# Row sums of squared differences on one core: two first loads of x instead of four, and the result stored in two halves from two queues

## The chip, the core and the metric

The kernel runs on one core of a Trainium2 chip. The metric is the device time of one execution in microseconds. Before the change it is 84.13 us, the median of three runs (84.11 to 84.14).

## What is computed

Two float32 arrays of 1024 x 4096 come in; for each row the sum of the squared differences goes out, 1024 float32 values.

```python
def reference(x, y, axis):          # x, y: (1024, 4096) float32, axis = -1
    return np.sum((x - y) ** 2, axis=axis).astype(np.float32)
```

Each input is 16.8 MB, so 33.55 MB are read and 4 KB are written. Nothing is read twice.

## The kernel before

Each of the 128 partitions holds R = 8 rows of D = 4096 elements, so x and y are each seen as 128 x 32768 (lines 60 and 61), and a partition's share is one contiguous stretch of memory. The work goes along these 32768 columns. On the chip, X and Y each have room for 24576 columns (`H = 6 * D`); the columns above that are written over those of the first two rows once these have been squared.

**Loads.** `xw` and `yw` (lines 72 and 73) are the widths of the pieces in which x and y are loaded; one piece is one DMA of 128 partitions (`load`, line 108) with a semaphore of its own. All loads are issued by SP, on one queue, in the order of the list `order`: before each piece of y come the pieces of x that it needs. The first piece of y is 16256 columns wide, so the first four pieces of x (512, 1536, 4096 and 10240 columns, together 16384) stand ahead of it. These four are issued "early": `prog.early` moves them ahead of SP's Drain in the entry block, that is ahead of the barriers with which the program begins. The barriers let the other engines go on only when SP has come to them. The first piece of y and the later loads follow behind the barriers. As many loads as fit into the room are issued at once (up to the 8192-column pieces); the rest are issued when the square of the last piece of row 0, and then of row 1, is done (line 221 is SP's wait). SP's queue holds only so many transfers: an issue into a full queue lasts until there is room.

**Work.** For each piece of y, in order, DVE waits for the piece and for the pieces of x that it needs (`wait_loaded`, line 172), subtracts it from x in place (line 176), cut at the rows' ends and for some pieces halved. ACT squares each difference and adds it up along the row into one column of `parts` (line 182). A row that was done in several pieces is summed by DVE at its end (line 189). The very last piece, 128 columns, is squared on DVE itself (line 205), and then row 7 is summed. The semaphore `diffs` counts DVE's subtractions, `acts` ACT's squares, `sums` the results that are final.

**Store.** When all results are final, SP issues one DMA of 128 partitions x 8 values (line 233), with the semaphore `stored`. `close` clears the program's semaphores (line 44) and waits for `stored` (line 45). That wait is the last instruction of the program.

Engine names: DVE is VectorE, ACT is ScalarE, SP is SyncE, POOL is GpSimd. Line numbers are those of the kernel before.

Of the kernel before, what the change touches and what calls it, by code (L numbers as in the profile page):

```python
# [47 lines left out]
def kernel(tc, x, y, axis, out):  # L48
    nc = tc.nc
    P = nc.NUM_PARTITIONS  # L50
# [11 lines left out]
    ov = out.rearrange("(p r) -> p r", p=P)  # L62
# [5 lines left out]
    results = nc.alloc_sbuf_tensor("results", [P, R], F32).ap()  # L68

    xw = [512, 1536, 4096, 10240, 8192, 5472, 1280, 960, 320, 160]
    yw = [16256, 8192, 2624, 2784, 1344, 480, 480, 288]
    late, last = 128, 192
    LATE = 3
# [15 lines left out]
    prog = Program(nc, tc)  # L91
    stored = nc.alloc_semaphore("stored")
    diffs = prog.semaphore("diffs")
    acts = prog.semaphore("acts")
    sums = prog.semaphore("sums")
    n = dict(diffs=0, acts=0, sums=0)

    def home(c0, c1):
        h0 = c0 % H
        return slice(h0, h0 + c1 - c0)  # L100
# [5 lines left out]
    def load(landed, src, dst, name, c0, c1):  # L106
        sem = prog.semaphore("%s%d" % (name, len(landed)))
        nc.sync.dma_start(out=dst[:, home(c0, c1)], in_=src[:, c0:c1]).then_inc(sem, 16)  # L108
        landed.append(((c0, c1), sem))
# [7 lines left out]
        order.append((landed_y, yv, Y, "y", c0, c1))  # L117

    todo = list(order)
    for _ in range(4):  # L120
        load(*todo.pop(0))
    prog.early(mybir.EngineType.SP)
    while todo and todo[0][5] <= H:
# [63 lines left out]
    def complete(r):  # L187
        nc.vector.wait_ge(acts, squared[row_parts[r][-1]])
        nc.vector.tensor_reduce(  # L189
            out=results[:, r : r + 1],  # L190
            in_=parts_of(r, len(row_parts[r])),
            axis=mybir.AxisListType.X,
            op=add,
        ).then_inc(sums, 1)
        n["sums"] += 1

    for j, (c0, c1) in enumerate(ys):
        final = j == len(ys) - 1
        wait_loaded(c1, landed_y[j][1])
        for piece in pieces_of(j, c0, c1):  # L200
            sub(*piece)
            r = piece[0] // D
            if final:
                nc.vector.wait_ge(diffs, n["diffs"])
                nc.vector.tensor_tensor_reduce(  # L205
                    out=Y[:, home(*piece)],
# [22 lines left out]
                complete(r)  # L229
    complete(7)  # L230

    nc.sync.wait_ge(sums, n["sums"])
    nc.sync.dma_start(out=ov, in_=results).then_inc(stored, 16)
    prog.close(nc.sync, stored, 16)


# [33 lines left out]
```

## Time and profile before

| | |
|---|---|
| time of the profiled execution | 84.13 us |
| its span, first to last instruction | 82.80 us |
| around the span | 1.33 us |
| first load issued by SP | 0.00 us |
| the four early loads, from first issue to end of the last | 1.80 us |
| first load of y issued | 2.86 us |
| first subtraction on DVE | 41.04 us |
| one subtraction of 128 x 4096 | 4.42 us |
| one square of 128 x 4096 | 3.62 us |
| last subtraction ends | 80.82 us |
| store issued | 81.36 us |
| issue to landing of the store | 1.4 us |

All times within the execution count from the start of the span. The trace also has a record of every DMA packet: its start, its length and its size, not the engine that moved it. A load of 128 partitions appears as 128 packets, 8 for each of the 16 DMA engines, with one completion of 4 bytes for each engine behind them. In the chain that ended last, an entry "DMA Y<-in_y_dram" is the time from the issue of such a load to its landing, and "SPq" is time in which SP issued or waited.

### The profile page before, as it was taken

To read this page: it belongs to the slowest core of one execution; us is meant where nothing else is said; L and a number is where in the kernel's file an instruction comes from. 1 tells how busy PE (TensorE), PEld (TensorE's weight loads), DVE (VectorE), ACT (ScalarE), POOL (GpSimd) and SP (SyncE) were. 2 spreads that over 40 slices of the span, in tenths; PEclk is the share of its full clock that TensorE was granted. 3 is DMA by queue.
4 is the path that set the end of the run, shared out by engine and by line. 5 is a ranking of instruction groups with operands and counts; after the bars stand their busy time and mean duration, and the time that the engine had idled before them with its cause. 6 is when DMAs were issued, how large, how long until landed. Compare 5 with 4: busy or idle time off the path is not lost.

```text
span 82.8 us, 139 instructions
## 1 busy us (share of the span) xinstructions
DVE 36.8 (44%) x27; ACT 33.4 (40%) x41; POOL 0.2 (0%) x4
## 2 busy tenths in 40 slices
DVE  0000000000000000000199999999179996989992
ACT  0600000000000000000000979889796999899991
POOL 0000000000000000000000000000000000000000
DMA  5999997997999995699699989979999999999950
GB/s 137 393 452 419 455 613 317 396 554 317 503 503 503 503 503 220 283 503 503 285 475 507 412 348 507 443 332 491 412 391 465 389 411 424 430 408 416 395 195 2
DMA packets 3024, 33.56 MB, mean 405 GB/s; under 512 B 464, under 2 KB 1360, under 8 KB 2000
## 3 DMA queue, kind: packets, MB, share of 16 engines
q1 hardware_dynamic: 3024, 33.56, 95.7%
HBM read 33.55 MB, written 0.00 MB: 405 GB/s over the span
## 4 chain that ended last, share of the span: by engine, by line
DMA 59%; SPq 19%; DVE 12%; ACT 4%; issue 1%
DMA Y<-in_y_dram 59%; SPq L108 19%; DVE X L176 11%; ACT X L182 4%; DVE Y L205 0%; DVE results L189 0%; SPq L221 0%; DVE results L205 0%
## 5 line engine op out<-in xcount | busy, mean ns | idle before, releaser
L176 DVE TENSOR_TENSOR X<-X,Y 128x2048 f32<-128x2048 f32 (+10 forms) x21 | 36.3, 1779 | 44.5 <-DMA Y<-in_y_dram 44.3
L182 ACT ACTIVATE X<-X 128x2048 f32<-128x2048 f32 (+9 forms) x20 | 31.2, 1558 | 44.8 <-DVE X L176 44.8
L182 ACT ACTIVATION_READ_ACCUMULATOR X<-X 128x1 f32 x20 | 3.7, 186 | 0.0
L182 ACT ACT_TABLE_LOAD x1 | 1.3, 1283 | 2.9 <-PEq L19 2.9
L189 DVE TENSOR_REDUCE results<-parts 128x1 f32<-128x2 f32 (+2 forms) x4 | 0.4, 151 | 0.0
L205 DVE CUSTOM_DVE_ANT_0 Y<-X,parts 128x128 f32<-128x128 f32 x1 | 0.4, 353 | 0.0
L251 POOL MEMSET const-bfloat16-1.0<- 128x1 bf16 x1 | 0.1, 101 | 0.0
L251 POOL MEMSET const-uint8-127<- 128x1 uint8 x1 | 0.1, 101 | 0.0
L251 POOL MEMSET const-float32-0.0<- 128x1 f32 x1 | 0.1, 98 | 0.2 <-issue 0.2
L251 POOL MEMSET const-float32-1.0<- 128x1 f32 x1 | 0.1, 98 | 0.0
L205 DVE DVE_READ_ACCUMULATOR2_ANT results<- 128x1 f32 x1 | 0.1, 84 | 0.0
## 6 DMA issues: line engine op xcount, KB each, us to landing
Y<-in_y_dram SPq DMA_DIRECT2D x1, 8128.0 KB, 38.2
X<-in_x_dram SPq DMA_DIRECT2D x1, 5120.0 KB, 20.4
X<-in_x_dram SPq DMA_DIRECT2D x1, 4096.0 KB, 47.5
Y<-in_y_dram SPq DMA_DIRECT2D x1, 4096.0 KB, 56.7
X<-in_x_dram SPq DMA_DIRECT2D x1, 2736.0 KB, 13.3
X<-in_x_dram SPq DMA_DIRECT2D x1, 2048.0 KB, 8.8
Y<-in_y_dram SPq DMA_DIRECT2D x1, 1392.0 KB, 18.9
Y<-in_y_dram SPq DMA_DIRECT2D x1, 1312.0 KB, 16.1
```

Source lines behind the costliest of these rows:

```text
L108: nc.sync.dma_start(out=dst[:, home(c0, c1)], in_=src[:, c0:c1]).then_inc(sem, 16)
L176: nc.vector.tensor_sub(out=a, in0=a, in1=Y[:, home(c0, c1)]).then_inc(diffs, 1)
L182: nc.scalar.activation(out=a, in_=a, func=Square, accum_out=acc).then_inc(acts, 1)
L189: nc.vector.tensor_reduce(out=results[:, r : r + 1], in_=parts_of(r, len(row_parts[r])), axis=mybir.AxisListType.X, op=add,).then_inc(sums, 1)
L205: nc.vector.tensor_tensor_reduce(out=Y[:, home(*piece)], in0=X[:, home(*piece)], in1=X[:, home(*piece)], scale=1.0, scalar=parts_of(r, 1), ...
L251: nc = _bacc.Bacc("TRN2", target_bir_lowering=False, num_devices=1)
```

## The change

The four early loads of x become two, of 4096 and 12288 columns: the same 16384 columns, in the same place of the order. The store becomes two DMAs of 64 partitions: ACT issues the upper half and SP the lower half, each after its own wait for `sums`. ACT then increments a new semaphore, `begun`, and SP waits for it before the program's semaphores are cleared, among them `sums`, for which ACT waits. The last wait counts both halves (32 in place of 16).

```diff
-    xw = [512, 1536, 4096, 10240, 8192, 5472, 1280, 960, 320, 160]
+    xw = [4096, 12288, 8192, 5472, 1280, 960, 320, 160]
...
+    begun = prog.semaphore("begun")
...
-    for _ in range(4):
+    for _ in range(2):
         load(*todo.pop(0))
     prog.early(mybir.EngineType.SP)
...
+    half = P // 2
+    nc.scalar.wait_ge(sums, n["sums"])
+    nc.scalar.dma_start(out=ov[half:P], in_=results[half:P]).then_inc(stored, 16)
+    nc.scalar.sem_inc(begun, 1)
     nc.sync.wait_ge(sums, n["sums"])
-    nc.sync.dma_start(out=ov, in_=results).then_inc(stored, 16)
-    prog.close(nc.sync, stored, 16)
+    nc.sync.dma_start(out=ov[0:half], in_=results[0:half]).then_inc(stored, 16)
+    nc.sync.wait_ge(begun, 1)
+    prog.close(nc.sync, stored, 32)
```

## The prediction

> **What bounds the kernel now.** I read the page's engine shares and slices first, then the chain that ended last, then the transfers, and last the two places that the diff touches: the first microseconds and the end. The page:
>
> ```profile
> span 82.8 us, 139 instructions
> ...
> DVE 36.8 (44%) x27; ACT 33.4 (40%) x41; POOL 0.2 (0%) x4
> ...
> DMA  5999997997999995699699989979999999999950
> GB/s 137 393 452 419 455 613 317 396 554 317 503 503 503 503 503 220 283 503 503 285 475 507 412 348 507 443 332 491 412 391 465 389 411 424 430 408 416 395 195 2
> ...
> q1 hardware_dynamic: 3024, 33.56, 95.7%
> ...
> DMA 59%; SPq 19%; DVE 12%; ACT 4%; issue 1%
> ```
>
> No compute engine is busy half the time; the 16 DMA engines are busy 95.7% of it. So the time is: a start, 33.55 MB at a steady rate, and an end. The 19% of SPq in the chain is SP held in one issue (11.12 us from 58.42) because earlier transfers fill its queue; the transfers themselves go on meanwhile.
>
> The steady rate comes from two rows of the transfers:
>
> ```profile
> Y<-in_y_dram SPq DMA_DIRECT2D x1, 8128.0 KB, 38.2
> X<-in_x_dram SPq DMA_DIRECT2D x1, 5120.0 KB, 20.4
> ...
> out_dram<-results SPq DMA_DIRECT2D x1, 4.0 KB, 1.4
> ```
>
> The 5120 KB piece of x was issued at 1.37 us and landed at 21.8; the 8128 KB piece of y was issued at 2.86 and landed at 41.0, straight behind it. 8.323 MB in 19.2 us is 433 GB/s. At that rate the first 8.389 MB (the x columns of the edit) need 19.4 us, yet they landed at 21.8: the stream is 2.4 us late. Of this, 1.0 us lies ahead of the first packet (issue at 0.00, first packet in the trace's packet records at 1.00) and 0.37 us between an engine's last packet and its completion. The remaining **1.07 us** is all that any other order of loads could recover. The windows show where it goes (start:end, length, the engines' busy time, clock, DMA share, GB/s):
>
> ```profile
> 0.90:1.30 0.40, 0.00 (x0) 0.00 (x0) 0.00 (x0) 1.00 0.75 133
> 1.30:1.70 0.40, 0.00 (x0) 0.00 (x0) 0.00 (x0) 1.00 0.61 179
> 1.70:2.10 0.40, 0.00 (x0) 0.00 (x0) 0.00 (x0) 1.00 1.42 425
> 2.10:2.50 0.40, 0.00 (x0) 0.00 (x0) 0.00 (x0) 1.00 0.86 271
> 2.50:2.90 0.40, 0.00 (x0) 0.04 (x1) 0.00 (x0) 1.00 0.90 369
> ...
> 9.00:21.00 12.00, 0.00 (x0) 0.00 (x0) 0.00 (x0) 1.00 1.00 434
> ```
>
> Two dips: 133 and 179 GB/s while the 512-column load runs, and 271 as the 1536-column load begins.
>
> The end, from the chain in order of time and the timeline:
>
> ```profile
> 69.58 10.65 DMA Y<-in_y_dram
> 80.23 0.02 issue
> 80.25 0.57 DVE X L176 x2
> 80.83 0.03 issue
> 80.85 0.35 DVE Y L205
> ...
> 81.36 0.35 SPq L233 DMA_DIRECT2D out_dram<-results  x1
> ```
>
> The last loads land, 1.1 us of compute follows, the store is issued at 81.36 and is home 1.4 us later. The profiled execution took 84.13 us for a span of 82.80, so 1.33 us lie around it; its time equals the median of the three runs, and I take every sum from 84.13.
>
> **The loads, removed part.** Two of four early loads go; the bytes stay. (a) In the packet records each load gives each DMA engine 8 packets and one completion. Undisturbed packets start 80 ns apart at 2 KB, 231 ns at 6 KB, 607 ns at 16 KB: 27.2 bytes per ns plus 4.7 ns a packet; a completion adds 6 ns. A load fewer saves 8 x 4.7 + 6 = 44 ns on each engine, two save **0.09 us**.
>
> (b) Some early packets are far slower: 2 KB ones take up to 539 ns against a usual 84, 6 KB ones up to 989 against 234. Summed over what is usual and divided by 16 engines, that is 0.22 us per engine in the first load, 0.24 in the second, 0.02 in the third. Later small packets (512 to 1920 bytes at the end) have none of it. The trace can't say whether the excess belongs to the small early loads or to the first microseconds of reading. Bounds: all 0.46 goes, or all stays, or a first load of 16 KB rows is worse still: if the dip of 0.9 to 1.7 us (156 GB/s on average) also filled 1.7 to 2.5, where 348 were moved, 0.8 x (348 - 156) / 433 = 0.36 us more are lost. I take **0.24**: the second load's excess goes, since most of its slow packets are the first of that load, and with 4096 columns first the next load begins only near 6 us, when the third load of now shows almost nothing; the first load's stays, since some first load must meet the cold start. A large first row could also hide its stall, as one 16 KB packet covers 607 ns; this I leave for a rival.
>
> (c) SP's early block ends sooner: the removed issues stood 0.47 us apart, so SP's drain, now at 1.85 us, comes near 0.9. The other engines reach that barrier by 0.5 us, so the barriers, the table load of ACT (now at 2.86) and the first load of y (2.86) all move some 0.9 us forward. Worth nothing: that load queues behind 19 us of x, and ACT has nothing to square before 45 us. DVE has two waits fewer in a stretch where it idles until 41.04. The queue that holds SP later holds it as before, and the load so held lands at 79.98, 10 us after SP began to issue it.
>
> **Does an earlier stream reach the end?** DVE waits for DMA before the pieces of 2048, 1312 and 736 columns (idle 2.13, 0.77 and 0.36 us), and its last subtractions begin 0.02 us after landings at 79.73 and 80.23. Every run of compute thus hangs on a landing and moves with it; up to about 0.36 us nothing else is late instead. Beyond that the 736-column run starts to lean on DVE.
>
> **The store, added part.** Now: issue 0.35 us, first packet 0.84 after the issue began, all 128 packets and 16 completions within 0.19, then 0.37 to the last landing. After: 64 rows on each queue, 4 packets per engine each. SP's own half saves 4 packets at about 18 ns, 0.07 us, but the other half's 4 packets and a second completion go to the same 16 engines, so if both come together nothing is saved; the lower bound is -0.1. ACT is idle since 81.14, and behind its wait stands only its issue and the increment of "begun". SP's wait for "begun" has the semaphore clear (0.07 us) and the final wait behind it: it must end by about 82.7, and ACT's issue should end near 81.75, so 0.9 us of cover hides it. What no row shows is ACT's queue at work. Its nearest row is the first transfer of SP's queue: issue 0.38, first packet after 1.00, that is 0.15 later than the store's 0.84. The far row is the spacing of two issues of one queue, 0.47, should both queues be served one after the other; cold as well, 0.62. I take the near one, 0.15 less 0.07: **+0.08**, bounds -0.1 and +0.62.
>
> The Trainium skill speaks against this half of the change: "DMA: Bandwidth & Descriptors", section "Rules for kernel authors", says not to bother with two transfers to disjoint partition halves, as both use the same 16 engines. By that rule the store brings 0 at best; going instead by halved packets it would bring -0.07. No row here has two queues; the packet counts agree with the rule.
>
> Sum: -0.09 - 0.24 + 0.08 = -0.25, so **83.88 us**.
>
> **Rivals.**
> - *All of the excess goes* (0.46, long first packets cover the stall): -0.09 - 0.46 + 0.08 = -0.47, 83.66. For it: third-load packets show almost none. Against: the dip may be the memory's own start, and DVE leaning in takes some.
> - *The excess stays* because it belongs to the first 2.5 us whatever is read: -0.09 + 0.08, 84.12, no change. For it: the slow packets of different engines end near the same two moments, 1.6 and 2.6 us. It is also the case in which the change does little of what it says: the store is in two, but its packets share the engines.
> - *ACT's queue is late*, at the store: its packets come 0.47 to 0.62 after SP's, and the final wait counts both halves. With the loads at -0.09 and 0.47 paid: +0.38; with 0.62 and the loads at -0.33, +0.29; about 84.45. It decides the sign once ACT's half lands 0.33 us later than the store does now. For it: nothing orders a first use cheaply. Against: SP's own first use cost only 0.15.
> - *A worse start*: all 16 engines begin on long rows and the first dip lasts to 2.5 us: +0.36 - 0.09 + 0.08 = +0.35, 84.48. For it: 16 KB packets at the third load still show one of 866 ns against 611. Against: that sum is only 0.02 per engine.
>
> **How the numbers follow.** Chances: forecast 0.27 (its own range 83.75 to 83.96), all goes 0.17, stays 0.23, ACT late 0.20, worse start 0.13. About 0.2% (0.17 us) is what a measurement of this kernel can tell from no change. Faster 0.44, same 0.23, slower 0.33. The range 83.5 to 84.5 takes in the centres of all cases; left out are a store later by more than a cold issue and a fully recovered start.
>
> **What would show it.** Loads: the first 8.389 MB land near 21.5 instead of 21.8, GB/s over 350 from 2.1 us on, first y issue near 1.9; if they land at 21.7 the excess stayed, past 21.9 the start got worse. Store: two issues within 0.05 us of each other after the last reduction, and a last landing 1.4 to 1.5 us after; if the landing takes 1.8 or more, ACT's queue is the cause, and if its issue alone takes over 0.8 us, the hidden "begun" comes out as well. I am wrong if the two 16 KB-and-up loads stall like the small ones, or ACT's first transfer costs far more than SP's first.

## The result: 84.70 us, 0.6% slower

Four runs after the change give a median of 84.70 us (84.57 to 84.73); four of the kernel before, beside them, 84.13 (84.11 to 84.17). The ratio is 1.0064, 95% interval 1.0047 to 1.0082. The profiled execution took 84.73 us for a span of 83.39, so 1.34 us lie around the span, as before. The loss is in the span: 0.59 us.

### The profile page after: what moved, and what is told of

Same layout as the page of the kernel before. It is cut to its first block, busy times and chain, and to the rows that moved or that the text cites. A ratio compares the mean times of both kernels' runs of the same rounds, so it can differ in the third digit from the quotient of the medians.

```text
span 83.4 us, 138 instructions
## 1 busy us (share of the span) xinstructions
DVE 36.7 (44%) x27; ACT 33.4 (40%) x41; POOL 0.2 (0%) x4
## 4 chain that ended last, share of the span: by engine, by line
DMA 63%; SPq 16%; DVE 12%; ACT 4%; issue 1%
DMA Y<-in_y_dram 63%; SPq L109 16%; DVE X L177 11%; ACT X L183 4%; DVE Y L206 0%; DVE results L190 0%; SPq L222 0%; DVE results L206 0%
```

## The profile after

The page, same lines as before the change (a second queue, q10, is ACT's):

```profile
span 83.4 us, 138 instructions
...
DVE 36.7 (44%) x27; ACT 33.4 (40%) x41; POOL 0.2 (0%) x4
...
DMA  5999998888999999299889969998998999999930
GB/s 126 409 464 409 660 448 377 377 377 377 499 499 499 499 499 468 94 437 499 377 377 503 503 283 472 503 393 362 430 493 367 400 423 446 400 422 418 390 117 2
...
q1 hardware_dynamic: 2672, 33.56, 95.2%
q10 hardware_dynamic: 80, 0.00, 0.0%
```

The steady part is the same work by the same 16 engines. Single slices such as 94 or 660 are no place to look for 0.6 us: a slice is 2.1 us long, and one packet of the largest load takes 2.4 us. The two ends are.

The start, by windows (start:end, length, busy time of the engines, clock, DMA share, GB/s), first of after, then of before:

```profile
0.90:1.70 0.80, 0.00 (x0) 0.00 (x0) 0.00 (x0) 1.00 1.48 307
1.70:2.50 0.80, 0.00 (x0) 0.57 (x1) 0.00 (x0) 1.00 0.64 266
2.50:4.10 1.60, 0.00 (x0) 0.71 (x1) 0.00 (x0) 1.00 0.90 379
0.90:4.10 3.20, 0.00 (x0) 1.28 (x1) 0.00 (x0) 1.00 0.98 333
```

```profile
0.90:1.70 0.80, 0.00 (x0) 0.00 (x0) 0.00 (x0) 1.00 0.68 156
1.70:2.50 0.80, 0.00 (x0) 0.00 (x0) 0.00 (x0) 1.00 1.14 348
2.50:4.10 1.60, 0.00 (x0) 1.24 (x1) 0.00 (x0) 1.00 1.02 419
0.90:4.10 3.20, 0.00 (x0) 1.24 (x1) 0.00 (x0) 1.00 0.96 335
```

A window counts a packet whole where it starts (the 307 GB/s of after's first 0.8 us are 15 packets of 16 KB), so its figures jump with the size of the packets. With each packet of the records spread over its length, the three stretches give 138, 244 and 419 GB/s after the change and 138, 324 and 396 before; the whole 3.2 us give 305 and 313. So the first dip is as deep as before and lasts longer. The single packets say how: 15 of the 16 engines' first 16 KB packets took 1069 to 1678 ns where 611 is usual. The excess over the usual lengths, per engine, is 0.65 us in after's first load; in the three first loads of before it was 0.22, 0.24 and 0.02, together 0.49 before rounding. The first 8.389 MB landed at 21.89 us, 0.08 later than before.

The first issues and the store in the timeline, and the transfers of the store:

```profile
0.00 0.86 SPq L109 DMA_DIRECT2D X<-in_x_dram  x2
...
1.92 0.33 SPq L109 DMA_DIRECT2D Y<-in_y_dram  x1
1.93 1.28 ACT L183 ACT_TABLE_LOAD   x1 [1.93 <-PEq L19]
```

```profile
81.20 0.16 DVE L190 TENSOR_REDUCE results<-parts 128x1 f32<-128x8 f32 x1
81.39 0.53 SPq L239 DMA_DIRECT2D out_dram<-results  x1
81.39 0.54 ACTq L236 DMA_DIRECT2D out_dram<-results  x1
```

```profile
out_dram<-results SPq DMA_DIRECT2D x1, 2.0 KB, 1.7
out_dram<-results ACTq DMA_DIRECT2D x1, 2.0 KB, 2.0
```

The first load of y left SP 0.94 us earlier (1.92 against 2.86 us) and nothing came of it. The store was issued at 81.39, 0.03 us later than before. But each issue lasted 0.53 to 0.54 us instead of 0.35; SP's half landed 1.70 us after its issue, ACT's 1.97, where the whole store had taken 1.41. So 0.03 + 0.56 = 0.59 us: **the whole loss stands behind the last reduction.** What has to be explained is why half a store takes longer than a whole one, and why the second half takes longer still.

## The experiments

The theory after the first reading: two issues at the same time disturb each other. The rivals: ACT's queue is slow when first used; 64 rows are slow by themselves; the loads share the loss.

### The two parts of the change by themselves

Loads as before, with the store of the change:

> The kernel before with the store in two halves alone; the loads stay four. Main theory: the whole loss is the store (from store issue to last landing 1.97 us after the change, 1.41 before, +0.56; the store was issued only 0.03 later). Expected 84.13 + 0.56 = 84.69. Rival, that loads and store share the loss about evenly: 84.4. In the profile: both issues last about 0.53 us and the packets of ACT's half come about 0.27 us after those of SP's half.

Measured: 84.80 us, ratio 1.0071 (1.0051 to 1.0090). Issue and transfers:

```profile
81.21 0.53 SPq L238 DMA_DIRECT2D out_dram<-results  x1
81.21 0.55 ACTq L235 DMA_DIRECT2D out_dram<-results  x1
```

```profile
out_dram<-results SPq DMA_DIRECT2D x1, 2.0 KB, 1.7
out_dram<-results ACTq DMA_DIRECT2D x1, 2.0 KB, 2.0
```

The last landing came 1.97 us after the issue and ACT's first packet 0.28 after SP's: the whole loss, with none of the load edit.

The load edit alone:

```diff
-    xw = [512, 1536, 4096, 10240, 8192, 5472, 1280, 960, 320, 160]
+    xw = [4096, 12288, 8192, 5472, 1280, 960, 320, 160]
...
-    for _ in range(4):
+    for _ in range(2):
```

> The kernel before with two early loads (4096 and 12288 columns) alone; the store stays whole. Main theory: the packet overhead saved (0.09 us) is eaten by a longer stall of the first 16 KB packets (0.65 us of excess per engine in the profile of after, against 0.49 in the first three loads of before): 84.13 + 0.0 to 0.1, so 84.13 to 84.25. Rival, the prediction's own loads term of -0.33: 83.80. Rival, the loads share the loss: 84.4.

Measured: ratio 0.9983 (0.9965 to 1.0001), that is -0.14 us (-0.29 to +0.01). In its profile the excess of the first load is 0.63 us per engine, and the store is issued at 81.30 against 81.36. The loads carry none of the loss, and the -0.33 of the prediction lies outside the interval. Whether they bring a tenth of a microsecond stays open at this precision. The traces give no sign that they do: in the two profiles with this edit the first 8.389 MB landed at 21.76 and 21.89 us; in nine of the thirteen profiles with four loads it was 21.57 to 21.81, and in the other four one DMA engine or more fell behind.

### Whose fault in the store: the queue, the number of issues, or the 64 rows

The whole store from ACT, SP only waiting:

```diff
-    nc.sync.wait_ge(sums, n["sums"])
-    nc.sync.dma_start(out=ov, in_=results).then_inc(stored, 16)
+    nc.scalar.wait_ge(sums, n["sums"])
+    nc.scalar.dma_start(out=ov, in_=results).then_inc(stored, 16)
+    nc.scalar.sem_inc(begun, 1)
+    nc.sync.wait_ge(begun, 1)
```

> The kernel before with its one whole store of 128 rows issued by ACT in place of SP, SP only waiting for its landing; no second issue beside it. Theory 'two issues at once disturb each other': ACT alone takes about what SP took, issue near 0.35 us and landing 1.4 us after it, so 84.13 to 84.25. Theory 'ACT's queue, unused until then, is slow': the landing comes 1.8 to 2.0 us after the issue, 84.5 to 84.7.

Measured: ratio 0.9989 (0.9970 to 1.0008).

```profile
81.22 0.37 ACTq L234 DMA_DIRECT2D out_dram<-results  x1
```

First packet 0.87 us after the issue, last landing 1.44: within 0.03 us of SP's. ACT's queue, used for the first time in the program, is not slow with 128 rows. That rival falls.

One half alone, on SP:

```diff
-    nc.sync.dma_start(out=ov, in_=results).then_inc(stored, 16)
+    nc.sync.dma_start(out=ov[0:half], in_=results[0:half]).then_inc(stored, 16)
```

> The kernel before, SP storing the lower 64 partitions only; the upper half of the output is left out. Theory 'two issues at once': this one issue, alone, lasts 0.35 us again and lands in 1.3 to 1.4 us, 84.05 to 84.13. Theory 'an issue of 64 rows is slow by itself': the issue lasts about 0.53 us and lands 0.3 us later than the whole store, 84.4.

Measured: ratio 1.0031 (1.0009 to 1.0054), some 0.26 us slower with half the rows and one issue.

```profile
81.27 0.53 SPq L234 DMA_DIRECT2D out_dram<-results  x1
```

```profile
out_dram<-results SPq DMA_DIRECT2D x1, 2.0 KB, 1.7
```

The same 0.53 and 1.70 as with ACT beside it. My theory of two issues disturbing each other falls for SP's half: nothing was beside it. First packet 1.17 us after the issue, where the whole store has 0.84.

The other half alone, on ACT (the edit of the whole store from ACT, with partitions 64 to 127 only):

> The kernel before, ACT alone storing the upper 64 partitions; the lower half of the output is left out. Theory 'the second queue waits for the first': alone, ACT's half lands as SP's half did alone, first packet 1.17 us after the issue, last landing 1.70 after it. Rival 'ACT is slow with 64 rows': first packet 1.45 us after the issue, landing 1.97, as in the kernel with both halves.

Measured in one execution: 84.42 us; issue 0.53 us, first packet 1.19 after it began, last landing 1.71. ACT's half alone lands like SP's half alone. In the kernel with both it lands 0.26 later, so it is held up by SP's half or its issue. There ACT's first packet starts 1.44 us after the issue; SP's last completion was sent at 1.34.

### Is it the count of rows?

In these SP alone stores a part of the result, and the number, the place or the width of the rows differs; each was executed once.

> The kernel before, SP storing only the lowest 32 partitions; the rest of the output is left out. If any transfer of fewer than 128 rows takes one slower way: issue 0.53 us, first packet 1.17 after it, as with 64 rows. If the cost grows as the rows get fewer: issue over 0.6 us and first packet past 1.3. If it falls again with the rows: under 0.5 and under 1.1.

> The kernel before, SP storing only the lowest 96 partitions; the rest of the output is left out. So far 128 and 32 rows were issued in 0.35 and 0.36 us, 64 rows in 0.53. If 64 rows alone are slow (a count peculiar to it): issue about 0.36 us, first packet 0.85 after it. If counts that do not fill the partitions evenly are slow in general: 0.53 and 1.17.

> The kernel before, SP storing the middle 64 partitions (32 to 95) only; the rest of the output is left out. If the count of 64 is what is slow: issue 0.53 us, first packet 1.17 after it, landing 1.70, as with the lower and the upper 64. If it is the place, a half that ends on the boundary of 64: about 0.36, 0.85 and 1.38.

> The kernel before, SP storing only 4 of the 8 values of the lower 64 partitions: 64 rows of 16 bytes that are not contiguous in the output; the rest is left out. If the count of 64 rows is slow: issue 0.53 us, first packet 1.17 after it. If it was the 2048 contiguous bytes: 0.35 and 0.85.

> The kernel before, SP storing the lowest 48 partitions only; the rest of the output is left out. 32 and 96 rows were issued fast. If only 64 is slow: issue 0.36 us, first packet 0.86 after it. If counts around 64 share it: 0.5 or more and 1.15 or more.

All times in us; first packet and landing count from the start of the issue:

| rows stored by one issue | issue | first packet | last landing |
|---|---|---|---|
| 128 (before) | 0.35 | 0.84 | 1.41 |
| 96 | 0.36 | 0.86 | 1.40 |
| 64, lower half | 0.53 | 1.17 | 1.70 |
| 64, upper half, by ACT | 0.53 | 1.19 | 1.71 |
| 64, partitions 32 to 95 | 0.59 | 1.23 | 1.75 |
| 64, 4 of 8 values | 0.53 | 1.17 | 1.69 |
| 48 | 0.36 | 0.85 | 1.35 |
| 32 | 0.36 | 0.86 | 1.35 |

The issue in the profiles of 32 rows, of 96 rows and of partitions 32 to 95, in this order:

```profile
81.30 0.36 SPq L233 DMA_DIRECT2D out_dram<-results  x1
```

```profile
81.81 0.36 SPq L233 DMA_DIRECT2D out_dram<-results  x1
```

```profile
81.35 0.59 SPq L233 DMA_DIRECT2D out_dram<-results  x1
```

Of the five counts tried only 64 is slow, in each of the three places, on either queue, and whether or not the rows are contiguous in the output: about 0.17 us more in the issue, 0.33 until the first packet, 0.29 until the landing. The bytes are not it either, since 4 of 8 values are half as many. With 32 and 48 rows the landing is 0.06 us earlier than with 128. What in the chip makes 64 slow the traces do not show: the packets that do come are as many as they should be (64 and 16 completions) and as short (7 to 9 ns).

### What the second queue costs without 64 rows

Two halves by columns, each 128 rows of 4 values:

```diff
+    half = R // 2
+    nc.scalar.dma_start(out=ov[:, half:R], in_=results[:, half:R]).then_inc(stored, 16)
...
+    nc.sync.dma_start(out=ov[:, 0:half], in_=results[:, 0:half]).then_inc(stored, 16)
```

> The kernel before with the store in two halves by columns instead of rows: SP stores the first 4 values of all 128 partitions, ACT the last 4. Each half then is a transfer of 128 rows again. Theory 'two losses add up: a 64-row store begins 0.33 us later by itself, and the second queue's packets come 0.28 us after the first's': only the second is left, issues of about 0.35 us, SP's first packet 0.84 after its issue, ACT's about 0.28 later, last landing 1.65 to 1.7 after the issue, 84.4. Rival 'everything is due to 64 rows': landing at 1.4 us, 84.13. Rival 'two queues cost the same whatever their rows': 84.7.

Measured: ratio 1.0034 (1.0000 to 1.0069).

```profile
81.55 0.35 SPq L238 DMA_DIRECT2D out_dram<-results  x1
81.56 0.38 ACTq L235 DMA_DIRECT2D out_dram<-results  x1
```

```profile
out_dram<-results SPq DMA_DIRECT2D x1, 2.0 KB, 1.4
out_dram<-results ACTq DMA_DIRECT2D x1, 2.0 KB, 1.6
```

Short issues again, and ACT's first packet 0.05 us after SP's, not the 0.28 I expected. Yet the last landing is at 1.58, 0.17 later than with one store. The semaphore records show where it arises: 32 completions instead of 16 arrive one after the other, mostly 8 to 10 ns apart, from 1.25 to 1.58 us; the 16 of one store take from 1.25 to 1.41.

Is it a queue at the one semaphore? The same with a semaphore for each half:

```diff
-    ...in_=results[:, half:R]).then_inc(stored, 16)
+    ...in_=results[:, half:R]).then_inc(stored_act, 16)
...
+    nc.sync.wait_ge(stored_act, 16).then_inc(stored_act, -16)
```

> The store in two halves by columns, as in col_split, but each half counted on a semaphore of its own. In col_split ACT's packets came only 0.05 us after SP's, yet the last landing was 0.17 later than with one store; the 32 completions arrive at least 8 ns apart, one after the other. If this is a queue at the one semaphore: two semaphores bring the last landing back to 1.42 to 1.47 us after the issue and the time to 0.0 to 0.1 above the kernel before. If completions are taken one at a time whatever the semaphore: 1.58 again and 0.15 to 0.2 above it.

Measured: ratio 1.0017 (0.9991 to 1.0044). SP's 16 completions came from 1.25 to 1.41 us, ACT's from 1.43 to 1.58: all of ACT's behind all of SP's, and the last at 1.58 again. A queue at the one semaphore is ruled out. The time alone would not have told these apart; the records do. They also show how the 0.17 is made up: ACT's completions are sent 0.05 us after SP's, and then need 0.48 us to land where SP's need 0.36 to 0.37. That they wait for SP's fits this order, but what they wait at is not shown.

Two parts by rows, neither of 64 rows (`half = 96` in the store of the change):

> The kernel before with the store in two parts by rows, SP 96 and ACT 32; both queues, both issues, the wait for 'begun' and the 32 completions are as in the change, only no part has 64 rows. Theory 'the count of 64 carries the loss': issues of 0.36 to 0.38 us, ACT's packets 0.05 us after SP's, last landing 1.58 us after the issue because 32 completions come one after the other; 0.17 us above the kernel before, 84.3. Rival 'a split by rows loses 0.56 whatever the counts': 84.7.

Measured: ratio 1.0013 (0.9989 to 1.0037), that is +0.11 us (-0.09 to +0.31).

```profile
81.97 0.36 SPq L238 DMA_DIRECT2D out_dram<-results  x1
81.97 0.40 ACTq L235 DMA_DIRECT2D out_dram<-results  x1
```

```profile
out_dram<-results SPq DMA_DIRECT2D x1, 3.0 KB, 1.4
out_dram<-results ACTq DMA_DIRECT2D x1, 1.0 KB, 1.6
```

Last landing 1.58 us after the issue, as foretold: both queues, both issues and the wait for `begun` are there, and most of the loss is not. (In this profile one DMA engine's part of the third load landed 0.8 us after the others', near 10 us, hence the late store; the landing counts from the issue and is not touched by that.) So the 0.56 us of the change are 0.29 for 64 rows, and 0.27 for the second half, which comes behind the first where both have 64 rows. In the other forms a second transfer lands 0.17 later, most of it in its completions.

### The stall at the start

First a small load and then one large, whole store:

```diff
-    xw = [512, 1536, 4096, 10240, 8192, 5472, 1280, 960, 320, 160]
+    xw = [512, 15872, 8192, 5472, 1280, 960, 320, 160]
...
-    for _ in range(4):
+    for _ in range(2):
```

> The kernel before with the 16384 early columns in two loads of 512 and 15872, the store whole. It keeps the small first load and removes two loads. Theory 'the excess at the start stays whatever the sizes, about 0.5 to 0.65 us per engine': only packet overhead goes, 84.13 - 0.05 to - 0.1. Theory 'a small load keeps the stall short, and long first packets make it longer': the excess falls under 0.4 us and the time to 83.95 or less. Rival 'growing sizes are what avoids the stall': excess over 0.65 and 84.2 or more.

Measured: ratio 0.9974 (0.9939 to 1.0009), too wide to tell from no change. Excess per engine: 0.24 us in the small load and 0.34 in the large, together 0.58, as the theory that the excess stays had it.

The two big loads after a tiny one that has landed, whole store (the widths of `xw` are those of the change):

```diff
     todo = list(order)
+    nc.sync.dma_start(out=scratch, in_=xv[:, 0:64]).then_inc(woken, 16)
+    nc.sync.wait_ge(woken, 16)
     for _ in range(2):
```

> The two big early loads of the change with the whole store; ahead of them SP loads 64 columns of x into a scratch tile and waits for them, so that the big loads meet DMA engines and a memory that have just been at work. The whole program starts about 1.9 to 2.1 us later, 86.0 to 86.3; what counts is the excess of the first 16 KB packets over 611 ns, 0.63 to 0.65 us per engine without the scratch load. If the stall is a cold start: under 0.2 us. If it is 16 engines beginning on rows at the same offset at once: 0.5 us or more, as before.

Measured: 85.83 us in one execution, 1.70 above the kernel before and a little less than foretold, because the first packets of the big loads start at 2.68 instead of 1.00. Windows of this run:

```profile
0.90:1.70 0.80, 0.00 (x0) 0.00 (x0) 0.00 (x0) 1.00 0.18 41
1.70:2.50 0.80, 0.00 (x0) 0.00 (x0) 0.00 (x0) 1.00 0.00 0
2.50:4.10 1.60, 0.00 (x0) 0.50 (x1) 0.00 (x0) 1.00 1.06 276
```

The tiny load (256-byte packets, 15 to 18 ns each) meets no stall; the first 16 KB packets after it take 731 to 1661 ns, an excess of 0.68 us per engine. So the stall is **not that of the program's first read**: it comes with the first large packets, also when a small load has landed 1.0 us earlier. The last packet of the tiny load had ended 1.3 us before them, so a stall after any such pause is not ruled out. That it comes from 16 engines beginning on their rows together fits, but was not tried by itself.

## Why the prediction was wrong, step by step

The forecast was 83.88, range 83.5 to 84.5; measured 84.70.

- **What bounds the kernel**: right. A stream, then a fixed end; a delay of the store's landing passed whole into the time (0.56 of the 0.59 us that the span grew by).
- **(a) Packet overhead, -0.09**: not seen by itself; it lies within the interval of the loads alone (-0.29 to +0.01), together with (b).
- **(b) Excess at the start, -0.24**: wrong. I took the second load's excess to go. Two big loads have 0.63 to 0.65 us of excess against 0.49 in before's profile, and against 0.29 to 0.52 in all thirteen profiles with four loads. The row I had, third-load packets with almost none, was of engines in the middle of a stream, not of engines that begin. The reason that I gave for keeping the first load's share, a cold start, found no support: the tiny load ahead, 1.3 us earlier, did not help. By the excess it lies between the rivals "the excess stays" and "a worse start"; by the time, nearest to "stays". Had only this term failed, at 0 in place of -0.24, the forecast would have been 84.12, which is inside the range.
- **(c) Earlier barriers, 0**: right. The first load of y was issued at 1.92, nothing followed. Two readings beside it were not right. The load held in SP's queue landed at 79.98, which is 10 us after its issue ended and 21.6 us, not 10, after SP began to issue it. And SP was not held as before: before, one issue of 11.12 us from 58.42, with 11 earlier loads not yet landed; after, issues of 1.66, 5.21 and 2.69 us from 57.50, with 9 not yet landed at the first, and later one of 5.56. So it is not a fixed number of loads that fills the queue; what does is open. It cost nothing that shows: the load that the last subtractions wait for landed at 80.29 against 80.23 us.
- **The store, +0.08**: this is the step that failed; measured it is +0.56. It had two terms. The 0.15 for an unused queue is 0.03 in the run with the whole store from ACT; what delays the second half instead is the first half, by 0.27. The -0.07 for four packets fewer on SP's half is +0.29: I scaled a transfer by its packets and took for granted that the issue and the time to the first packet do not depend on the number of rows. Even the scaling was off: the 18 ns a packet stand in no record. By the rule under (a) a packet of 32 bytes costs 5.9 ns, and the first completion of the store follows its first packet by 45 ns, which fits 8 such packets; four fewer are 0.02 us. No row of the trace showed a transfer of anything but 128 rows, and I did not list that as unknown.
- **The wait for `begun`**: right. SP cleared its semaphores at 82.0 us and then waited for the landing until 83.4 us.
- **The rule of the Trainium skill** ("DMA: Bandwidth & Descriptors", "Rules for kernel authors": two transfers to disjoint partition halves are not worth it): right in direction, and it should have weighed more than 0 against -0.07. The two halves of 64 rows did come one behind the other here, 0.27 us between their first packets; the parts of 96 and 32 rows overlapped, 0.04 apart. But the rule speaks of no price, and neither the slow 64 rows nor the time for twice the completions is in it. What the same page says under "Why a DMA increments its semaphore by 16 and not by 1", that each engine posts a completion of its own, agrees with the 16 records per store here, and 32 for two.
- **The rivals**: "ACT's queue is late" named the right place and the right sign, and its 0.47 for one queue served after the other stands against 0.27 measured. But it held a cold or second queue guilty and missed that the first half is late too, so it is partly luck that its 84.45 lies near the result. The sign I set for it, a landing of 1.8 us or more after the issue, did appear (1.97), yet the conclusion I tied to it, that ACT's queue is the cause, would have been half wrong. Of the two signs that I am wrong, the big loads did stall like the small ones; ACT's first transfer did not cost far more than SP's (0.03 us with the whole store).
- **The range**: my own bounds, +0.62 for the store and +0.36 - 0.09 for the loads, reach 85.02. I cut the range to 84.5 around the rivals' centres, and so left out a value that my bounds allowed.

Open: what makes 64 rows slow, why the second 64-row half comes behind the first, what the completions of a second transfer wait for, and what the first large packets wait for.

## What to carry to other kernels

A small store at the very end is nearly all latency: here, of the 1.41 us from issue to landing, only 0.19 lie between its first packet and its last completion sent; the rest is the issue, the time to the first packet, and the way to the landing. Cutting it in two saved no latency in any form tried and added 16 completions, and each must be counted before the program ends. Before a transfer is given another number of rows, measure one of that shape: a shape that the trace does not have is an unknown, even when it is half of one that it has. And when bounds have been worked out, let the range reach them.

## What was not expected of the hardware

- A store of 64 rows is issued in 0.53 to 0.59 us and its first packet starts 1.17 to 1.23 us after the issue began; from SP, 32, 48, 96 and 128 rows take 0.35 to 0.36 and 0.84 to 0.86.
- Completions of two overlapping transfers arrive one behind the other, mostly 6 to 10 ns apart, and with a semaphore for each transfer those of the second came behind all of the first: 32 of them end 0.17 us later than 16.
- ACT's queue issues its first transfer of the program nearly as fast as SP issues the same store (0.37 against 0.35 us; landing 1.44 against 1.41).
- A stream that begins with 16 KB packets loses 0.63 to 0.68 us per engine in them, even when a small load landed 1.0 us before.
